# The last moved pair of the second attention is cast half a tile later, GpSimd takes half of two low parts, and the last early output step stands between the last transposes

## The chip, the cores and the metric

The program runs on one core of one Trainium2 chip. The metric is the device time of one execution in microseconds (us); lower is better. A core has five instruction queues that matter here: PE (TensorE, matmuls and transposes), ACT (ScalarE), DVE (VectorE), POOL (GpSimd) and SP (SyncE, which only issues DMAs). Each works through its own instructions in the order in which they were written into its queue, and waits for others by semaphores.

## The reference, cut to what matters

Two layers over 1024 rows of width 1024: differential attention, then multi-head latent attention (MLA), each with a gate, an output projection and a residual. The change is at the end of the second one:

```python
sc = (jnp.einsum('bqhd,bkhd->bhqk', qn, k_nope, preferred_element_type=f32)
      + jnp.einsum('bqhr,bkr->bhqk', qp, k_pe, preferred_element_type=f32)) * scale
p = jax.nn.softmax(sc, axis=-1)
return jnp.einsum('bhqk,bkhd->bqhd', p.astype(v.dtype), v)
...
o = o.reshape(b, s, MLA_WIDTH) * jax.nn.silu(z)
return o @ w_out
```

There are 8 heads with 1024 queries and 1024 keys each. All is float32. The kernel gets there by splitting an operand x into a high part (a cast to the matmul's float32r) and a low part (x minus the high part), and adding three matmuls: high x high, high x low, low x high (`mm3`, L203 to L205).

## The kernel before

**Tiles.** `attn1` (from L1839) goes through one head in 8 tiles of 128 queries. A counter `now[0]` runs on over the heads, so tile n is tile n - 8h of head h: head 6 has the tiles 48 to 55, head 7, the last, 56 to 63. For a tile, `scores1` does ten score matmuls into PSUM (the tile `s1`, printed as `s`; six on `kn`, then four on `kps`), DVE takes the negated row maximum (`nm`, L433), ACT the exponential (`e`, L436).

**Transposes.** The weights e have to be transposed before the product with v (`pv`). There are two ways:
- by PE, in two halves of four 128x128 transposes (`tr`, L414, `Tail.turn(0)` and `turn(1)`). ACT casts the half to its high part (`pth<-tr`, L416), DVE subtracts for the low part (`ptl<-tr`, L419). There is one PSUM buffer for `tr`, so the next half on PE can begin only when DVE has done the low part of the one before. Tile n's first half is transposed after the scores of tile n+1, its second half amid the scores of tile n+2, between their six `kn` matmuls and their four `kps` matmuls.
- by moving ("moved pair", class `Mate`), in heads 0 to 6 for tiles 0, 1 and for tiles 4, 5: DVE transposes 32x32 blocks (`eT`, L1047), the result goes to DRAM (`pS`) and comes back rearranged (`pr`, four DMAs, `Mate.fetch`). Then `Mate.high` has ACT cast two blocks of 128x1024 (`pth<-pr`, L1065), one for each half kh of the keys, and `Mate.low` has the low parts done (`ptl<-pr`): by DVE (L1084), and for the very last pair, whose `high` runs with `closing[0]` set, by GpSimd for kh = 0 (L1081).

**When.** `settle` sets the steps by tile number: a pair that ends in tile n is fetched at n+2, its `high` at n+4 (`SPLIT_AT`), its `low` at n+5, its product at n+6 (one later for head 6's first pair). So head 6's first pair (tiles 48, 49) has `high` at tile 53, `low` at 54 and its product at 56; its last pair (tiles 52, 53) has `high` at 57, `low` at 58 and its product at 59. In heads 0 to 6 these steps are written right behind the tile's scores; in head 7 behind all of the tile's other work. Head 7 has no moved pairs. While it runs, `closing[0]` is set and the casts on ACT and the exponentials keep the order in which the program has them (`pin_last`); PE's order is fixed throughout (`pin`). Instructions on DVE, POOL and SP are put in order by the scheduler, with hints (`behind`, `in_turn`).

**The end.** During head 7, `extra1` also loads what the output projection needs and, by the table `PRE1` (one entry a tile from 56 on, then three for the end), does early steps of the output projection: six matmuls `oacc` for one head (`Pre.step`). After tile 63, `run_tails` does the last three half transposes (tile 62's second half, tile 63's first and second) with an `extra1` call behind each, and then tile 63's product:

```python
        prev.turn(1)
        fill(0)
        last.turn(0)
        prev.pv(0)
        prev.pv(1)
        fill(1)
        last.turn(1)
        fill(2)
        last.pv(0)
        last.pv(1)
```

Here `fill(i)` is `extra(8 + i)`, and `prev.pv` does nothing, since the product of two tiles is done with the second of them.

## Time and profile before

| | us |
|---|---|
| three runs | 1411.88, 1419.05, 1419.73 |
| their median | 1419.05 |
| the profiled execution, its own time | 1413.83 |
| its span, first to last instruction | 1412.0 |
| PE busy in the span | 1374.9 |

The profiled execution took 1.83 us more than its span. The scores of the tiles that matter start on PE at (tile: us) 54: 1251.87, 55: 1254.88, 56: 1257.54, 57: 1264.99, 58: 1271.05, 59: 1280.08, 60: 1287.13, 61: 1293.18, 62: 1299.24, 63: 1304.53; the last product starts at 1318.34.

A row of the timeline has its start, its length, the engine, the line, the operation with output and input, and in brackets the idle time of the engine before it and what ended that. A group "x2" is two instructions, from the start of the first to the end of the second. Matmul rows overlap: a 128x512 matmul is shown some 0.4 us long, but the next one starts about 0.23 us after it.

### The profile page before, as it was taken

What the parts mean: (1) busy time and instruction counts of PE and PEld (TensorE: products, weight loads), DVE (VectorE), ACT (ScalarE), POOL (GpSimd) and SP (SyncE); (2) the same over time, 40 slices, a digit from 0 to 9 for tenths busy, and PEclk for the clock granted to TensorE, in tenths of its full rate; (3) what the DMA queues carried; (4) which work ended last, traced back from release to release, by engine and by line L of the source; (5) the groups of instructions that cost most, each with busy time, mean ns of one, the idle gap of its engine ahead of it and who ended that gap; (6) DMA issues with size and microseconds to landing.
All of it is one profiled execution on the core that took longest, in us unless ns stands there. A gap on an engine that the chain in (4) does not pass through costs nothing.

```text
span 1412.0 us, 20440 instructions
## 1 busy us (share of the span) xinstructions
PE 1374.9 (97%) x7254; PEld 1150.0 (81%) x7254; DVE 936.7 (66%) x1365; ACT 740.3 (52%) x1290; POOL 610.6 (43%) x484
## 2 busy tenths in 40 slices
PE   9999899999999999999999999999999999998997
PEld 7778688888888888787778878888888888887886
DVE  7756687676777767678445787346777776764455
ACT  6623366666565655566443654345555555644342
POOL 4415164646564646462563235513142432313662
PEclk9999999999999999999999999999999999999999
DMA  9877723233333232336672222448688787776663
GB/s 352 262 226 233 237 66 103 79 103 83 105 85 95 80 96 81 97 87 221 219 240 97 97 90 90 126 146 261 164 223 248 213 240 195 204 214 214 226 213 129
DMA packets 147736, 230.98 MB, mean 164 GB/s; under 512 B 19121, under 2 KB 70449, under 8 KB 147634
## 3 DMA queue, kind: packets, MB, share of 16 engines
q1 hardware_dynamic: 147634, 229.68, 53.5%
q8 instruction: 57, 0.93, 0.3%
q14 instruction: 45, 0.37, 0.1%
HBM read 145.79 MB, written 60.23 MB: 146 GB/s over the span
## 4 chain that ended last, share of the span: by engine, by line
PE 78%; DMA 7%; DVE 6%; issue 3%; ACT 3%; SPq 2%; POOL 1%; ACTq 0%; POOLq 0%; DVEq 0%
PE acc L203 9%; PE acc L205 9%; PE acc L204 9%; PE s L1831 8%; PE s L905 7%; PE tr L414 6%; PE pv L204 4%; PE pv L205 4%; PE pv L203 4%; PE oacc L204 3%; PE oacc L205 3%; PE oacc L203 3%; PE zacc L203 1%; PE zacc L205 1%; PE zacc L204 1%
## 5 line engine op out<-in xcount | busy, mean ns | idle before, releaser
L433 DVE TENSOR_REDUCE nm<-s 128x1 f32<-128x1024 f32 x192 | 234.0, 1219 | 87.8 <-PE s L905 66.6
L416 ACT CAST pth<-tr 128x512 fp32r<-128x512 f32 x200 | 117.4, 587 | 212.8 <-PE tr L414 211.9
L436 ACT ACTIVATE e<-s,nm 128x1024 f32<-128x1024 f32 x128 | 143.2, 1119 | 94.6 <-DVE nm L433 94.2
L419 DVE TENSOR_TENSOR ptl<-tr,pth 128x512 fp32r<-128x512 f32 x200 | 137.2, 686 | 75.8 <-ACT pth L416 75.7
L254 POOL TENSOR_TENSOR wl<-wraw,wh 128x512 fp32r<-128x512 f32 (+2 forms) x82 | 102.7, 1254 | 170.4 <-ACT wh L253 162.8
L203 PE MATMUL acc<-h0h,wh 128*128 128x512 f32 x360 | 151.6, 421 | 1.8 <-DVE v_hl L393 1.7
L203 PE MATMUL pv<-pth,vt 128*128 128x256 f32 x512 | 146.4, 286 | 0.0
L204 PE MATMUL pv<-ptl,vt 128*128 128x256 f32 x512 | 145.2, 284 | 0.1
L205 PE MATMUL pv<-pth,vt 128*128 128x256 f32 x512 | 144.5, 282 | 0.0
L205 PE MATMUL acc<-h0h,wl 128*128 128x512 f32 x360 | 143.3, 398 | 0.1
L204 PE MATMUL acc<-h0l,wh 128*128 128x512 f32 x360 | 142.4, 396 | 0.0
L414 PE MATMUL tr<-ident,e 128*128 128x128 f32 x800 | 120.9, 273 | 10.1 <-DVE ptl L419 10.0
L414 PEld LDWEIGHTS tr<-ident,e 128*128 128x128 f32 x800 | 96.2, 140 | 41.6 <-DVE ptl L419 16.3
L1234 POOL TENSOR_TENSOR wol<-wor,woh 128x512 fp32r<-128x512 f32 x64 | 86.6, 1372 | 77.4 <-ACT woh L1233 71.4
L204 PEld LDWEIGHTS pv<-ptl,vt 128*128 128x128 f32 x512 | 97.2, 190 | 5.1 <-DVE ptl L419 0.4
L203 PEld LDWEIGHTS pv<-pth,vt 128*128 128x128 f32 x512 | 97.0, 189 | 4.5 <-ACT pth L416 0.4
L205 PEld LDWEIGHTS pv<-pth,vt 128*128 128x128 f32 x512 | 97.6, 191 | 0.1
L905 PE MATMUL s<-ks,qa 128*128 128x512 f32 x256 | 82.7, 403 | 6.0 <-ACT e L436 3.0
L913 DVE SCALAR_TENSOR_TENSOR e<-s,z,e 128x1024 f32<-128x1024 f32 x64 | 82.1, 1283 | 2.1
L355 POOL TENSOR_TENSOR rp_sw<-rp_sw,sinT 128x512 f32<-128x512 f32 x42 | 55.3, 1316 | 62.8 <-DMA rp_sw<-rp_raw 57.6
L205 PEld LDWEIGHTS acc<-h0h,wl 128*128 128x128 f32 x360 | 68.3, 190 | 16.4 <-POOL wl L254 0.6
L905 PE MATMUL s<-ks,qb 128*128 128x512 f32 x256 | 81.1, 396 | 0.0
(632 smaller groups left out, 3442.2 us busy)
## 6 DMA issues: line engine op xcount, KB each, us to landing
ada<-in_ada_ss SPq DMA_DIRECT2D x32, 512.0 KB, 6.4
wraw<-in_w_s SPq DMA_DIRECT2D x64, 256.0 KB, 2.8
vS<-v_hl SPq DMA_DIRECT2D x32, 512.0 KB, 5.0
vt<-vS SPq DMA_DIRECT2D x32, 512.0 KB, 5.0
wor<-in_w_out SPq DMA_DIRECT2D x64, 256.0 KB, 4.2
pS<-eT SPq DMA_DIRECT2D x28, 512.0 KB, 2.9
pr<-pS SPq DMA_DIRECT2D x56, 256.0 KB, 6.2
rp_sw<-rp_raw SPq DMA_DIRECT2D x168, 64.0 KB, 2.0
```

The lines of the kernel that those rows point to most:

```text
L203: pin(PE.matmul(psum, ah, bh, start=first, stop=False))
L204: pin(PE.matmul(psum, ah, bl, start=False, stop=False))
L205: mm = PE.matmul(psum, al, bh, start=False, stop=last)
L254: sub = (lo_on or (V if pair_of else G)).tensor_sub(l_[:, :n], raw[:, :n], f32v(h_[:, :n]))
L414: pin(PE.transpose(tr[:, j, :], p[:, kt * P : (kt + 1) * P], ident))
L416: cp = S.copy(pth[kh][:, :, dst], tr)
L419: mk["V"] = V.tensor_sub(ptl[kh][:, :, dst], tr, f32v(pth[kh][:, :, dst])).ins
L433: mk["V"] = V.reduce_max(nm, s_ps, axis=AX.X, negate=True).ins
L436: ex = S.activation(e, s_ps, AF.Exp, bias=nm, scale=1.0, accum_out=zs)
L905: PE.matmul(s_ps[:, kc * HF : (kc + 1) * HF], src[:, c, ql], KS[h][kc][:, c, :], start=fst, stop=not fst)
L1234: in_turn(G.tensor_sub(lo, raw, f32v(hi)))
L1831: pin(PE.matmul(s_ps[:, kc * HF : (kc + 1) * HF], lhs, rhs(kc), start=i == 0, stop=i == 4))
```

## The change

Three edits.
- `Mate.high` in head 7 (that is the last moved pair's, at tile 57) does nothing itself but leaves its work, now called `spread`, in a list `swing`. `scores1` of tile 58 runs it amid the scores, right after the second half transpose of tile 56. `low` stays at tile 58, behind its other work.
- Both of head 6's pairs now have their kh = 0 low part done by GpSimd, in `spread`, and their kh = 1 low part by DVE, in `low`. Before, this held for the last pair alone, and both were issued in `high` then; the first pair's two low parts were both DVE's.
- `PRE1` has its last early step one place earlier: between tile 63's first half transpose and its second, not behind the second.

```diff
-PRE1 = (0, 0, 1, 0, 0, 0, 1, 1, 1, 0, 1)
+PRE1 = (0, 0, 1, 0, 0, 0, 1, 1, 1, 1, 0)
...
-            self.done = False
+            self.onG = int(c["h"] == NH - 2)
...
         def high(self):
+            if closing[0]:
+                swing.append(self.spread)
+            else:
+                self.spread()
+
+        def spread(self):
             self.pt = alloc_pt(self.c["pt"])
             for kh in range(2):
-                r, (hi, _) = self.views(kh)
+                r, (hi, lo) = self.views(kh)
                 with behind("S"):
                     cp = S.copy(hi, r)
                     pin_last(cp)
                     last = cp.ins
+                if kh < self.onG:
+                    in_turn(G.tensor_sub(lo, r, f32v(hi)))
             mk["S"] = last
-            if closing[0]:
-                self.low(G)
-            else:
+            if not closing[0]:
                 mk["H"] = last
 
-        def low(self, eng=V):
-            if eng is V and self.done:
-                return
-            self.done = True
-            for kh in range(2):
+        def low(self):
+            for kh in range(self.onG, 2):
                 r, (hi, lo) = self.views(kh)
-                if eng is G and kh == 0:
-                    in_turn(G.tensor_sub(lo, r, f32v(hi)))
-                else:
-                    with behind("V"):
-                        V.tensor_sub(lo, r, f32v(hi))
-
-    tails, hooks = [None, None], []
+                with behind("V"):
+                    V.tensor_sub(lo, r, f32v(hi))
+
+    tails, hooks, swing = [None, None], [], []
...
-            if i == SPL1 and tails[0]:
-                tails[0].turn(1)
+            if i == SPL1:
+                if tails[0]:
+                    tails[0].turn(1)
+                while swing:
+                    swing.pop(0)()
```

What this moves in the queues. ACT around tiles 57 and 58, before. The first row is the cast of tile 56's first half, the `pth<-pr` pair is the last moved pair's, the `pth<-tr` behind it is tile 56's second half, and `s1_12870` are the scores of tile 58:

```order
L416 CAST pth_12826<-tr_12830 128x4x128
L1884 CAST bc_s_12520<-o1_12781 128x512
L1065 CAST pth_12851<-pr_12659 128x1024
L1065 CAST pth_12852<-pr_12659 128x1024
L1233 CAST woh_12859<-wor_12783 128x512
L416 CAST pth_12827<-tr_12877 128x4x128
L436 ACTIVATE e_12890,zz1_12725<-s1_12870,nm_12888 128x1024
```

The same place after the change (tile 58's scores are now `s1_12862`):

```order
L416 CAST pth_12826<-tr_12830 128x4x128
L1887 CAST bc_s_12520<-o1_12781 128x512
L1233 CAST woh_12851<-wor_12783 128x512
L416 CAST pth_12827<-tr_12869 128x4x128
L1071 CAST pth_12876<-pr_12659 128x1024
L1071 CAST pth_12877<-pr_12659 128x1024
L436 ACTIVATE e_12889,zz1_12725<-s1_12862,nm_12887 128x1024
```

The two moved casts went behind `woh` and behind the cast of tile 56's second half, and still stand ahead of tile 58's exponential.

DVE at the same place, before; `nm_12888` is tile 58's maximum, `ptl_12829<-tr_12877` the low part of tile 56's second half, `ptl_12828<-tr_12892` and `ptl_12829<-tr_12925` those of tile 57's halves:

```order
L433 TENSOR_REDUCE nm_12888<-s1_12870 128x1
L1084 TENSOR_TENSOR ptl_12854<-pr_12659,pth_12852 128x1024
L419 TENSOR_TENSOR ptl_12829<-tr_12877,pth_12827 128x4x128
L419 TENSOR_TENSOR ptl_12828<-tr_12892,pth_12826 128x4x128
L419 TENSOR_TENSOR ptl_12829<-tr_12925,pth_12827 128x4x128
L433 TENSOR_REDUCE nm_12936<-s1_12918 128x1
```

And after:

```order
L419 TENSOR_TENSOR ptl_12829<-tr_12869,pth_12827 128x4x128
L433 TENSOR_REDUCE nm_12887<-s1_12862 128x1
L419 TENSOR_TENSOR ptl_12828<-tr_12891,pth_12826 128x4x128
L1084 TENSOR_TENSOR ptl_12879<-pr_12659,pth_12877 128x1024
L419 TENSOR_TENSOR ptl_12829<-tr_12925,pth_12827 128x4x128
L433 TENSOR_REDUCE nm_12936<-s1_12918 128x1
```

Tile 56's low part moved ahead of tile 58's maximum, and the moved pair's low part from ahead of it to two places behind it. On POOL the first pair's low part is new, at tile 53, and the last pair's went from ahead of the first `wol<-wor` to behind it. On SP the load of head 7's second half of v (`vt`) went from behind the loads of `o1a3` and `o1a4` to ahead of them.

DVE at tiles 54 and 55, before; `nm_12645` is tile 54's maximum, `nm_12675` tile 55's, and the row behind that the low part of tile 54's first half:

```order
L433 TENSOR_REDUCE nm_12645<-s1_12634 128x1
L1084 TENSOR_TENSOR ptl_12596<-pr_12457,pth_12594 128x1024
L1084 TENSOR_TENSOR ptl_12597<-pr_12457,pth_12595 128x1024
L1777 SCALAR_TENSOR_TENSOR qn_l_12656<-acc_12566,qn_h_12655 128x512
L433 TENSOR_REDUCE nm_12675<-s1_12664 128x1
L419 TENSOR_TENSOR ptl_12681<-tr_12683,pth_12679 128x4x128
```

And after:

```order
L433 TENSOR_REDUCE nm_12646<-s1_12635 128x1
L1084 TENSOR_TENSOR ptl_12597<-pr_12457,pth_12595 128x1024
L433 TENSOR_REDUCE nm_12675<-s1_12664 128x1
L1777 SCALAR_TENSOR_TENSOR qn_l_12656<-acc_12566,qn_h_12655 128x512
L419 TENSOR_TENSOR ptl_12681<-tr_12683,pth_12679 128x4x128
```

One of the two low parts left DVE, and `qn_l` went behind tile 55's maximum.

PE after tile 63, as one piece of the difference; the `tr` row with x8 is tile 63's two halves, `o1a3` and `o1a4` are the last two early steps, `pv` the last product:

```order
 L204 MATMUL oacc<-wol,o1a3h 128x512
 L205 MATMUL oacc<-woh,o1a3l 128x512
-L414 MATMUL tr<-ident,e 128x128 x8
+L414 MATMUL tr<-ident,e 128x128 x4
 L203 MATMUL oacc<-woh,o1a4h 128x512
 L204 MATMUL oacc<-wol,o1a4h 128x512
```

The last four transposes went behind the six matmuls of the early step, directly ahead of `pv`.

## The prediction

> **What bounds the kernel now.** I read the page first, for the engine that sets the time, then the list of waits for the stretch that the change touches, then its timeline row by row.

> ```profile
> PE 1374.9 (97%) x7254; PEld 1150.0 (81%) x7254; DVE 936.7 (66%) x1365; ACT 740.3 (52%) x1290; POOL 610.6 (43%) x484
> ...
> PE 78%; DMA 7%; DVE 6%; issue 3%; ACT 3%; SPq 2%; POOL 1%; ACTq 0%; POOLq 0%; DVEq 0%
> ```

> PE is busy in 97% of the span, and the chain that ended last runs over PE for 78% of it. The change takes no matmul away, so it can bring only what PE loses to waits and to a lower clock. From 1225 us to the end of the span, PE's list of waits has one line (total, times, longest):

> ```profile
> PE tr L414 <- DVE ptl L419: 6.9, 5, 3.7
> ```

> So 6.9 us is all there is to take in waits: five times PE stood before a half transpose until DVE had done the low part of the half before, which frees the one `tr` buffer. The timeline has the five:

> ```profile
> 1260.27 0.65 PE L414 MATMUL tr<-ident,e 128*128 128x128 f32 x4 [1.11 <-DVE ptl L419]
> ...
> 1277.66 0.63 PE L414 MATMUL tr<-ident,e 128*128 128x128 f32 x4 [3.71 <-DVE ptl L419]
> ...
> 1302.64 0.66 PE L414 MATMUL tr<-ident,e 128*128 128x128 f32 x4 [0.48 <-DVE ptl L419]
> ...
> 1306.27 0.66 PE L414 MATMUL tr<-ident,e 128*128 128x128 f32 x4 [0.22 <-DVE ptl L419]
> ...
> 1316.45 0.66 PE L414 MATMUL tr<-ident,e 128*128 128x128 f32 x4 [1.40 <-DVE ptl L419]
> ```

> In order these are tile 56, tile 58, tiles 62 and 63, and the last transpose. The three edits aim at the first, second and fifth. Behind the second stands a further loss:

> ```profile
> 1272.44 0.60 PE L414 MATMUL tr<-ident,e 128*128 128x128 f32 x4
> ...
> 1280.08 1.05 PE L1831 MATMUL s<-kn_h,qn_h 128*128 128x512 f32 x2
> ...
> 1282.47 0.60 PE L414 MATMUL tr<-ident,e 128*128 128x128 f32 x4
> ...
> 1300.64 0.60 PE L414 MATMUL tr<-ident,e 128*128 128x128 f32 x4
> ...
> 1304.53 0.61 PE L1831 MATMUL s<-kn_h,qn_h 128*128 128x512 f32 x2
> ```

> The same view by stretches of 10 us (the third number from the end is the granted clock):

> ```profile
> 1280.00:1290.00 10.00, 10.00 (x58) 8.67 (x57) 3.51 (x6) 2.86 (x5) 0.82 (x1) 0.89 0.55 192
> ```

> Two score matmuls take 1.05 us at 1280.08 and 0.61 us at 1304.53, and the clock was 0.89: after the long wait PE ran slowly for a while.

> **Edit 1, the casts half a tile later.** Why did tile 58 wait 3.71 us? ACT and DVE there:

> ```profile
> 1272.36 1.99 ACT L1065 CAST pth<-pr 128x1024 fp32r<-128x1024 f32 x2 [0.60 <-issue]
> ...
> 1274.78 0.58 ACT L416 CAST pth<-tr 128x512 fp32r<-128x512 f32 x1
> ...
> 1275.14 1.78 DVE L1084 TENSOR_TENSOR ptl<-pr,pth 128x1024 fp32r<-128x1024 f32 x1
> 1276.84 0.68 DVE L419 TENSOR_TENSOR ptl<-tr,pth 128x512 fp32r<-128x512 f32 x1
> ```

> The transpose of 1272.44 is tile 56's second half. Its cast came only at 1274.78, behind the two moved casts (and a `woh`), and its low part at 1276.84, behind the moved pair's low part. After the change both stand ahead of those. What the place then looks like, tile 62 shows: it has the same PE program (transpose, four `kps`, transpose, six `oacc`, six `kn` of the next tile, transpose) and no moved pair. There the three transposes start at 1300.64, 1302.64 and 1306.27, which is 5.63 us from first to last. At tile 58 they start at 1272.44, 1277.66 and 1282.47, which is 10.03. If tile 58 becomes like tile 62, the gain is 10.03 - 5.63 = **4.40 us**: 3.22 up to the second transpose (5.22 against 2.00), and 1.18 behind it, where the slow stretch goes. Does it go with the wait? No slow matmul follows the wait of 1.40 us or the shorter ones (0.61 at 1304.53, 0.48 and 0.28 behind 1316.45 below), so I take it that it does; if it came from something else, the term would be 3.2. [...]

> Do the casts now hurt elsewhere? They stand between the cast of tile 56's half and tile 58's exponential, and tile 62 shows the room there:

> ```profile
> 1301.28 0.59 ACT L416 CAST pth<-tr 128x512 fp32r<-128x512 f32 x1 [1.32 <-PE tr L414]
> ...
> 1303.81 1.12 ACT L436 ACTIVATE e<-s,nm 128x1024 f32<-128x1024 f32 x1 [1.95 <-DVE nm L433]
> ```

> ACT idles 1.95 us before the exponential, waiting for the maximum; the pair of casts takes 1.99 us by its row, some 1.9 from start to start of what follows. They just fit: 0 to 0.1 us. Of the DMA they no longer need anything: the four `pr` loads had landed when the casts began at 1272.36, and the casts now begin about 1.2 us later than that (0.6 behind the transpose of 1272.44 the cast of its half, 0.5 behind that the moved ones). GpSimd's kh = 0 low part:

> ```profile
> 1273.48 2.35 POOL L1081 TENSOR_TENSOR ptl<-pr,pth 128x1024 fp32r<-128x1024 f32 x1 [0.36 <-DMA o1a1l<-oS]
> ...
> 1306.09 1.28 POOL L1234 TENSOR_TENSOR wol<-wor,woh 128x512 fp32r<-128x512 f32 x1 [3.29 <-ACT woh L1233]
> ```

> It now comes behind a `wol` of 1.28 us, which fits before the first moved cast is done, and is finished some 4.6 us after tile 56's transpose; the product that needs it starts 6.9 after it (5.63, a transpose, four `kps`). DVE's kh = 1 low part now stands between the low parts of tile 57's two halves. With 1.78 us, as at 1275.14, it pushes the second of them and tile 59's maximum by half a microsecond. What that meets, tiles 59 and 60 show:

> ```profile
> 1284.34 1.21 DVE L433 TENSOR_REDUCE nm<-s 128x1 f32<-128x1024 f32 x1
> ...
> 1287.36 0.69 DVE L419 TENSOR_TENSOR ptl<-tr,pth 128x512 fp32r<-128x512 f32 x1 [0.30 <-ACT pth L416]
> ...
> 1288.53 0.60 PE L414 MATMUL tr<-ident,e 128*128 128x128 f32 x4
> ```

> Tile 59's maximum starts, exponential and cast follow, the low part is done at 1288.05, and PE wants the buffer at 1288.53: 0.48 us of slack. So the push is absorbed but for 0 to 0.1 us. I take **0.1 us** off for both.

> [...]

> **Edit 2, half of the first pair's low part on GpSimd.** Tile 56 waited for this row chain on DVE:

> ```profile
> 1255.53 2.35 DVE L1084 TENSOR_TENSOR ptl<-pr,pth 128x1024 fp32r<-128x1024 f32 x2
> 1257.80 0.69 DVE L1777 SCALAR_TENSOR_TENSOR qn_l<-acc,qn_h 128x512 fp32r<-128x512 f32 x1
> 1258.40 1.22 DVE L433 TENSOR_REDUCE nm<-s 128x1 f32<-128x1024 f32 x1
> 1259.53 0.68 DVE L419 TENSOR_TENSOR ptl<-tr,pth 128x512 fp32r<-128x512 f32 x1
> ```

> and the end of tile 55's scores on PE:

> ```profile
> 1256.72 0.63 PE L1831 MATMUL s<-kps,qpb 128*128 128x512 f32 x2
> ```

> One L1084 goes, so DVE is free at 1255.53 + 1.17 = 1256.70. Next is tile 55's maximum, whose scores end at 1257.35, so it runs 1257.40 to 1258.53 (start to start 1.13), then `qn_l` to 1259.13, then the low part, done 0.68 later at 1259.81 against 1260.21: **0.40 us**, not the 1.17 us that left DVE, because the scores are now late. If `qn_l` did not stand in between, it would be the whole 1.0; if GpSimd got in the way of the maximum, nothing: 0 to 1.0. GpSimd has the time:

> ```profile
> 1258.12 1.54 POOL L1864 TENSOR_TENSOR gz<-gz,bc_s 128x512 f32<-128x512 f32 x1 [8.99 <-DMA bc_s<-bc_d]
> ```

> It idled 8.99 us before this row; the new low part, 2.35 us long, lies inside that, and ends before DVE begins its own.

> **Edit 3, the early step between the last transposes.** The wait of 1.40 us at 1316.45 is bound by cast and low part of the transpose before, and nothing stood beside it. The six `oacc` that followed now fill it; they took 1316.87 to 1318.34, so they fit. What they covered is open then: the product's second half needs the last low part, and has only twelve `pv` ahead of it.

> ```profile
> 1316.87 0.48 PE L203 MATMUL oacc<-woh,o1a4h 128*128 128x512 f32 x1
> ...
> 1317.76 0.69 DVE L419 TENSOR_TENSOR ptl<-tr,pth 128x512 fp32r<-128x512 f32 x1 [1.37 <-ACT pth L416]
> ...
> 1318.34 0.28 PE L203 MATMUL pv<-pth,vt 128*128 128x256 f32 x1
> ```

> `pv` starts at 1316.87 then, its twelve take about 1.43, the first that needs the low part comes at 1318.42, and the low part ends at 1318.45: a wait of 0.1. So 1.40 - 0.1 = **1.3 us** (1.0 to 1.4). The step's own weights are there: the `wol` at 1306.09 (above) is its, and follows ACT's order when all comes earlier. Nothing waits on PE from there to the end by the list of waits, and the loads of the next weights and rows wait for that product, so they come earlier with it.

> **Sum.** 4.40 - 0.1 + 0.40 + 1.3 = 6.0 us. The profiled execution took 1413.83 us, which gives **1407.8**, say 1408. The three runs spread over 8 us, and their median of 1419.05 is 5.2 above the profiled execution, one of them 1.95 below it. I forecast for an execution like the profiled one, since only its rows can be argued with; if the new runs spread as the old ones did, their median is 1413.

> **The rivals.** (a) *Only a part comes.* SP now has head 7's second `vt` ahead of four `o1a` loads. Before, it was issued at 1285.45 (after tile 59's first twelve `pv`), landed 5.0 us later and was used at 1291.67:

> ```profile
> 1285.45 0.32 SPq L405 DMA_DIRECT2D vt<-vS  x1
> ...
> 1291.67 0.36 PE L203 MATMUL pv<-pth,vt 128*128 128x256 f32 x1
> ...
> vt<-vS SPq DMA_DIRECT2D x1, 512.0 KB, 5.0
> ...
> DMA to landing us min/median/max: 3.6/6.5/8.6
> ```

> It keeps 6.2 us, but four loads of 256 KB now crowd in behind it; at the worst landing of this stretch, 8.6, PE waits 2.4 us at tile 60. That gives 1410.2. For it: the slack is only 1.2 us. Against it: those four are issued later than it. The other part that may fall out is the slow stretch: if it stays without the wait, 1409.0.

> (b) *The wait moves to tile 59.* If the two casts begin late, tile 58's exponential, the cast of tile 57's half and the third transpose move with them, one for one: then 3.22 us come back there, and only 1413.83 - 6.0 + 3.2 = 1411.0 is left, or nothing if another slow stretch follows. Against it: 0.15 us of room, and work ahead of them that tile 62 shows on time.

> (c) *Slower.* The casts now stand ahead of tile 58's exponential in ACT's fixed order, so a late `pr` blocks the softmax itself. Before, the landing set when they began:

> ```profile
> 1258.05 2.60 SPq L1054 DMA_DIRECT2D pr<-pS x4
> ...
> DMA to landing us min/median/max: 3.4/7.4/11.4
> ```

> From the last issue, near 1260.2, they must land within some 13.5 us not to cost anything; 11.4 is the worst row. Every microsecond beyond is lost once, and beyond 19.5 the gain of 6.0 is gone; at 21 and with a new slow stretch of 1.2 it would be 1416.5. It needs the loads to be nearly twice as slow, while one competitor, `o1a0l`, now comes behind them.

> **How the numbers follow.** Forecast 0.68, (a) 0.19, (b) 0.09, (c) 0.04. The terms' bounds: at the least edit 1 brings 4.40 - 0.1 - 1.18 (the slow stretch stays) - 2.4 (`vt`) = 0.7, edit 2 nothing, edit 3 1.0, together 1.7; at the most edit 1 5.1 (tile 62's own two waits of 0.48 and 0.22 gone too), edit 2 1.0, edit 3 1.4, together 7.5. From the profiled execution that is 1406.3 to 1412.1. The runs lie from 1.95 below to 5.9 above it, which widens this to 1404.4 and 1418; the uppermost 2 us need the worst of every term in the longest of the runs, so the range is 1404.5 to 1416. One per cent, 14 us, is about what a measurement of this kernel can tell from no change. No case reaches it by its terms; faster by over 1% needs the spread of the runs on top: 0.05. Slower by over 1%: 0.02. Within: 0.93.

> **What would show it.** In the trace after: at tile 58 no wait over 0.6 us before the second transpose and no clock under 1.00 behind it; the three transposes 5.6 to 5.8 us apart in all; PE's wait at tile 56 near 0.7; `pv` right behind the last transpose with 0.1 us of wait inside. I am wrong if tile 59 or 60 gets a wait of over 1 us, if `pr` or `vt` is what ends a wait, or if the slow stretch shows up in another place.

## The result, and the profile after

| | before | after |
|---|---|---|
| median of 7 runs each, us | 1414.67 (1411.88 to 1419.73) | 1407.04 (1404.94 to 1409.20) |
| profiled execution, us | 1413.83 | 1405.69 |
| its span, us | 1412.0 | 1403.9 |

The ratio of after to before is 0.9955, with a 95% interval of 0.994 to 0.997. A second measurement (below) gave 0.9954, 0.9937 to 0.9972: the change saves some 6.4 us, less than half a per cent. The forecast was 1408.0.

The tile numbers in this text count from the second attention's first tile (`now[0]` itself runs on from the first layer, so that tile 58 here is 122 there). The page of the kernel after, its engines:

```profile
PE 1372.2 (98%) x7254; PEld 1148.3 (82%) x7254; DVE 933.8 (67%) x1364; ACT 740.5 (53%) x1290; POOL 612.9 (44%) x485
```

The matmuls are the same 7254. What went is waiting; PE's list of waits from 1225 us to the end (total, times, longest) now reads:

```profile
PE tr L414 <- DVE ptl L419: 2.1, 5, 0.7
```

It was 6.9 us with 3.7 as the longest. In PE's timeline the places are these, first tile 56, then the three transposes of tile 58 with a pair of score matmuls among them:

```profile
1257.22 0.66 PE L414 MATMUL tr<-ident,e 128*128 128x128 f32 x4 [0.68 <-DVE ptl L419]
...
1269.39 0.60 PE L414 MATMUL tr<-ident,e 128*128 128x128 f32 x4
...
1271.40 0.66 PE L414 MATMUL tr<-ident,e 128*128 128x128 f32 x4 [0.49 <-DVE ptl L419]
...
1273.29 0.62 PE L1831 MATMUL s<-kn_h,qn_h 128*128 128x512 f32 x2
...
1275.03 0.66 PE L414 MATMUL tr<-ident,e 128*128 128x128 f32 x4 [0.22 <-DVE ptl L419]
```

Tile 58's second wait fell from 3.71 to 0.49 us, the pair of score matmuls takes 0.62 us instead of 1.05, and the three transposes stand 5.64 us apart instead of 10.03. The granted clock (third number from the end) stays at full there:

```profile
1270.00:1280.00 10.00, 9.29 (x58) 7.72 (x58) 6.08 (x7) 6.81 (x11) 7.48 (x5) 1.00 0.58 203
```

At the end the last transpose no longer waits, and the product stands right behind it:

```profile
1307.01 0.66 PE L414 MATMUL tr<-ident,e 128*128 128x128 f32 x4
...
1309.07 0.66 PE L414 MATMUL tr<-ident,e 128*128 128x128 f32 x4
...
1312.55 0.39 PE L203 MATMUL oacc<-woh,o1a5h 128*128 128x512 f32 x1
```

The runs of one kernel spread over some 4 to 12 us, so the experiments are read by a **stretch** of the timeline: from tile 55's first score matmul to the first output matmul of `o1a5h`, behind the last product. It runs from 1254.88 to 1321.20 before (66.32 us) and from 1252.24 to 1312.55 after (60.31 us). All three edits lie in it.

### The profile page after: what moved, and what is told of

Same layout as the page of the kernel before. It is cut to its first block, busy times and chain, and to the rows that moved or that the text cites. A ratio compares the mean times of both kernels' runs of the same rounds, so it can differ in the third digit from the quotient of the medians.

```text
span 1403.9 us, 20442 instructions
## 1 busy us (share of the span) xinstructions
PE 1372.2 (98%) x7254; PEld 1148.3 (82%) x7254; DVE 933.8 (67%) x1364; ACT 740.5 (53%) x1290; POOL 612.9 (44%) x485
## 4 chain that ended last, share of the span: by engine, by line
PE 81%; DVE 6%; DMA 4%; ACT 3%; issue 3%; SPq 1%; POOL 1%; ACTq 0%; POOLq 0%; DVEq 0%
PE s L1831 9%; PE acc L203 9%; PE acc L205 9%; PE acc L204 9%; PE s L905 7%; PE tr L414 6%; PE pv L204 4%; PE pv L205 4%; PE pv L203 4%; PE oacc L203 4%; PE oacc L205 4%; PE oacc L204 4%; PE zacc L203 1%; PE zacc L205 1%; PE zacc L204 1%
## 5 line engine op out<-in xcount | busy, mean ns | idle before, releaser
L433 DVE TENSOR_REDUCE nm<-s 128x1 f32<-128x1024 f32 x192 | 233.9, 1218 | 84.8 <-PE s L905 65.1
L416 ACT CAST pth<-tr 128x512 fp32r<-128x512 f32 x200 | 117.5, 587 | 208.4 <-PE tr L414 207.5
L436 ACT ACTIVATE e<-s,nm 128x1024 f32<-128x1024 f32 x128 | 143.3, 1120 | 94.0 <-DVE nm L433 93.5
L419 DVE TENSOR_TENSOR ptl<-tr,pth 128x512 fp32r<-128x512 f32 x200 | 137.2, 686 | 74.3 <-ACT pth L416 74.3
L203 PE MATMUL acc<-h0h,wh 128*128 128x512 f32 x360 | 151.2, 420 | 1.3 <-DVE v_hl L393 0.9
L203 PE MATMUL pv<-pth,vt 128*128 128x256 f32 x512 | 146.4, 286 | 0.0
L414 PEld LDWEIGHTS tr<-ident,e 128*128 128x128 f32 x800 | 96.1, 140 | 38.3 <-DVE ptl L419 17.4
L414 PE MATMUL tr<-ident,e 128*128 128x128 f32 x800 | 121.0, 273 | 6.3 <-DVE ptl L419 6.1
L1234 POOL TENSOR_TENSOR wol<-wor,woh 128x512 fp32r<-128x512 f32 x64 | 86.8, 1375 | 75.7 <-ACT woh L1233 64.3
L203 PEld LDWEIGHTS pv<-pth,vt 128*128 128x128 f32 x512 | 97.0, 189 | 4.5 <-ACT pth L416 0.4
## 6 DMA issues: line engine op xcount, KB each, us to landing
ada<-in_ada_ss SPq DMA_DIRECT2D x32, 512.0 KB, 6.4
vS<-v_hl SPq DMA_DIRECT2D x32, 512.0 KB, 5.0
vt<-vS SPq DMA_DIRECT2D x32, 512.0 KB, 5.1
pS<-eT SPq DMA_DIRECT2D x28, 512.0 KB, 2.9
```

What stands on the lines that cost most here:

```text
L203: pin(PE.matmul(psum, ah, bh, start=first, stop=False))
L414: pin(PE.transpose(tr[:, j, :], p[:, kt * P : (kt + 1) * P], ident))
L416: cp = S.copy(pth[kh][:, :, dst], tr)
L419: mk["V"] = V.tensor_sub(ptl[kh][:, :, dst], tr, f32v(pth[kh][:, :, dst])).ins
L433: mk["V"] = V.reduce_max(nm, s_ps, axis=AX.X, negate=True).ins
L436: ex = S.activation(e, s_ps, AF.Exp, bias=nm, scale=1.0, accum_out=zs)
```

## The experiments

All were compared with the kernel before on the same chip. "Stretch" is worked out from the starts of those two rows in each kernel's profiled execution.

| kernel | stretch, us | ratio to before, 95% interval |
|---|---|---|
| before, three profiled executions | 66.32, 67.15, 67.08 | |
| after, two profiled executions | 60.31, 60.31 | 0.9955 (0.994 to 0.997), 0.9954 (0.9937 to 0.9972) |
| moved casts alone | 62.00 | 0.9976 (0.9964 to 0.9987) |
| GpSimd's share in the first pair alone | 65.45 | 0.9983 (0.9972 to 0.9993) |
| last tile's early step alone | 63.07 | 0.9976 (0.9962 to 0.999) |
| before, the wait filled | 64.46 | 0.9985 (0.9974 to 0.9996) |
| after, casts ahead of the half transpose | 62.97 | 0.998 (0.9967 to 0.9993) |
| after, low part all on VectorE | 61.85 | 0.9968 (0.9951 to 0.9985) |
| after, casts a whole tile later | 66.33 | 0.9992 (0.9977 to 1.0007) |
| after, three more moves, twice | 58.88, 58.90 | 0.9949 (0.9933 to 0.9966), 0.9941 (0.9925 to 0.9958) |

**The moved casts alone.** The change without its line of `PRE1`, and with the first pair's low part left to DVE:

```diff
-            self.onG = int(c["h"] == NH - 2)
+            self.onG = int(c["h"] == NH - 2 and qp == 2)
```

> The kernel before with the moved casts alone; GpSimd's share and the early step of the last tile stay as before. Theory (the three edits act at three separate waits and add up): the three transposes of tile 58 stand about 5.6 us apart in all instead of 10.0 and run at full speed, the wait of tile 56 stays at 1.1 us and the one before the last transpose at 1.4 us; the stretch from tile 55's first score matmul to the first output matmul of o1a5h is 66.32 - 4.4 = 61.9 us. Rival (the casts need GpSimd's new share or the step to pay): a wait stays at tile 58 or appears at tile 59, and the stretch is 63 to 65 us.

Its timeline on PE (tile 56, the three transposes of tile 58, the last transpose):

```profile
1260.34 0.66 PE L414 MATMUL tr<-ident,e 128*128 128x128 f32 x4 [1.11 <-DVE ptl L419]
...
1272.52 0.60 PE L414 MATMUL tr<-ident,e 128*128 128x128 f32 x4
1274.52 0.66 PE L414 MATMUL tr<-ident,e 128*128 128x128 f32 x4 [0.48 <-DVE ptl L419]
1278.15 0.66 PE L414 MATMUL tr<-ident,e 128*128 128x128 f32 x4 [0.22 <-DVE ptl L419]
...
1312.20 0.66 PE L414 MATMUL tr<-ident,e 128*128 128x128 f32 x4 [1.40 <-DVE ptl L419]
```

The three transposes are 5.63 us apart, while the waits of 1.11 and 1.40 are those of before. The stretch is 4.32 us shorter, close to the theory's 4.4, and the casts need neither of the other edits.

**GpSimd's share alone.** In the kernel before, the first pair's first half goes to GpSimd behind its cast:

```diff
-                r, (hi, _) = self.views(kh)
+                r, (hi, lo) = self.views(kh)
...
+                if kh == 0 and self.c["h"] == NH - 2 and not closing[0]:
+                    in_turn(G.tensor_sub(lo, r, f32v(hi)))
...
-            for kh in range(2):
+            for kh in range(int(self.c["h"] == NH - 2 and not closing[0]), 2):
```

> The kernel before with GpSimd taking the first half of the first pair's low part (the part due at tile 56) and nothing else. Theory: the wait of tile 56 falls from 1.1 to about 0.7 us, tile 58 keeps its 3.7 us wait and the slow matmuls behind it, and the stretch from tile 55's first score matmul to the first output matmul of o1a5h is 66.32 - 0.4 = 65.9 us. Rival (the wait of tile 56 shrank only because the casts had moved as well): the wait stays at 1.1 us and the stretch at 66.3 us.

```profile
1258.72 0.66 PE L414 MATMUL tr<-ident,e 128*128 128x128 f32 x4 [0.68 <-DVE ptl L419]
...
1270.88 0.60 PE L414 MATMUL tr<-ident,e 128*128 128x128 f32 x4
1275.71 1.08 PE L414 MATMUL tr<-ident,e 128*128 128x128 f32 x4 [3.31 <-DVE ptl L419]
1280.46 0.60 PE L414 MATMUL tr<-ident,e 128*128 128x128 f32 x4
```

Tile 56's wait falls to 0.68 by this edit alone. From the stretch's start to tile 58's first transpose it takes 17.13 us (1253.75 to 1270.88) against 17.56 before: 0.43 saved, as expected. But the stretch lost 0.87. The other 0.44 went at tile 58, which the edit does not touch: its wait was 3.31 instead of 3.71, and the slow matmuls began at once (four transposes in 1.08 us) and were over sooner.

**The early step alone.** `PRE1` as in the change, nothing else.

> The kernel before with the early step of the last tile put between its last two transposes and nothing else. Theory: the 1.4 us wait before the last transpose is filled, from the last tile's third transpose to the end of the output it takes 7.0 - 1.3 = 5.7 us, and the stretch from tile 55's first score matmul to the first output matmul of o1a5h is 66.32 - 1.3 = 65.0 us, with tile 58 as before. Rival (the step is only moved within a chain that the softmax's tail sets): the wait moves to the product's first matmul and the stretch stays at 66.3 us.

```profile
1270.65 0.60 PE L414 MATMUL tr<-ident,e 128*128 128x128 f32 x4
...
1275.48 0.63 PE L414 MATMUL tr<-ident,e 128*128 128x128 f32 x4 [3.31 <-DVE ptl L419]
...
1278.71 0.60 PE L414 MATMUL tr<-ident,e 128*128 128x128 f32 x4
...
1312.70 0.65 PE L414 MATMUL tr<-ident,e 128*128 128x128 f32 x4
...
1316.17 0.39 PE L203 MATMUL oacc<-woh,o1a5h 128*128 128x512 f32 x1
```

The last transpose does not wait, and from the last tile's first half transpose (1310.64) to the end of the stretch it takes 5.53 us, against 6.81 (1314.39 to 1321.20) before: 1.28 saved. The stretch, however, lost 3.25 us. The rest, 1.97, again is tile 58, which nothing had touched: 8.06 us between its outer transposes instead of 10.03. The wait of 3.31 us is there, and **no slow matmul follows it**. The clock in the 10 us around it:

```profile
1274.00:1284.00 10.00, 8.52 (x55) 7.74 (x56) 4.43 (x7) 4.12 (x8) 4.65 (x3) 1.00 0.58 221
```

Of the single edits then, the first by its stretch and the other two read where they act, 4.32 + 0.43 + 1.28 = 6.03 us, and the whole change 6.01. By their total times they give more (0.9976, 0.9983 and 0.9976, so some 9 us); the intervals of the second and third even leave out the terms read in the trace. What the rest of these times is, the runs don't settle; tile 58's slow matmuls, which came out shorter or not at all in these two profiles, are one candidate.

**Filling the wait.** In the kernel before, 14 matmuls with no use stand in tile 58's wait:

```diff
+N_FILL = 14
...
+        if between and now[0] == 122:
+            kn_ = KN[NH - 1][0][0]
+            pre1.fill(N_FILL, kn_[:, :P], kn_)
...
+            for _ in range(n):
+                pin(PE.matmul(self.accs[0], lhs, rhs, start=True, stop=True))
```

> The kernel before with 14 more matmuls (about 3.3 us on TensorE, into a bank that is overwritten later, so that nothing uses them) put into the 3.7 us wait of tile 58, ahead of its second transpose. Theory (TensorE's idle wait is what brings the slow matmuls behind it): the wait left is about 0.4 us, the pairs of score matmuls behind it run at 0.6 us instead of 1.05, the clock's share stays at 1.00 there, and the stretch from tile 55's first score matmul to the first output matmul of o1a5h is 66.32 - 1.2 = 65.1 us although TensorE has more to do. Rival (the slow matmuls come from something else, such as the transfers and the other engines' load at that place): the wait is filled, the pairs still take 1.05 us and the stretch stays at 66.3 us.

(The lines are shifted by one or more in this kernel.)

```profile
1277.56 3.35 PE L1255 MATMUL oacc<-kn_h 128*128 128x512 f32 x14
1281.12 0.63 PE L415 MATMUL tr<-ident,e 128*128 128x128 f32 x4 [0.22 <-DVE ptl L420]
```

3.35 us of matmuls more, the wait 0.22, full speed behind it (0.63 us for the four transposes), and a stretch 1.86 us shorter. PE's work is not what this place costs. The gain is 0.7 us over the theory's 1.2: the first two transposes are 0.30 us closer (4.92 against 5.22), and the second and third 1.55 (3.26 against 4.81). Tile 62, from which the 1.2 was taken, has 3.63 there, with a wait of 0.22 in it that does not arise here. On the cause of the slow matmuls it says less than I wanted, since the run before this one had none of them with its wait unfilled.

**The kernel before again.** So it was profiled twice more, unchanged.

> The kernel before, unchanged, profiled once more. Theory A (the slow matmuls behind tile 58's wait come with the wait in every execution): the wait is 3.3 to 3.7 us, the pairs of score matmuls behind it take 1.05 us, and the stretch from tile 55's first score matmul to the first output matmul of o1a5h is 66.3 us, or 65.9 where the wait is 3.3 us. Theory B (whether they come is a matter of when the wait falls, as the kernel with the last tile's step alone suggests, where a 3.31 us wait was followed by matmuls at full speed): in some executions the stretch is 64.3 to 64.8 us, with pairs of 0.62 us.

> The kernel before, unchanged, profiled a third time. As for the second time: 65.9 to 66.3 us for the stretch and 1.05 us pairs by theory A; by theory B 64.3 to 64.8 us and pairs of 0.62 us in some executions, and more than one length of stretch among the three.

The second execution at tile 58, with the low part of DVE that the wait ends on:

```profile
1272.57 0.60 PE L414 MATMUL tr<-ident,e 128*128 128x128 f32 x4
...
1275.27 1.38 DVE L1084 TENSOR_TENSOR ptl<-pr,pth 128x1024 fp32r<-128x1024 f32 x1
...
1277.40 1.09 PE L414 MATMUL tr<-ident,e 128*128 128x128 f32 x4 [3.31 <-DVE ptl L419]
...
1283.40 0.61 PE L414 MATMUL tr<-ident,e 128*128 128x128 f32 x4
```

10.83 us from first to last, 10.79 in the third execution. The wait was 3.31 in both; the 3.71 of the first was DVE's low part, 1.78 us long there and 1.38 here. To see the slow part, the same view in windows of half a microsecond at its two edges (third number from the end: the granted clock), the first execution:

```profile
1278.50:1279.00 0.50, 0.50 (x4) 0.85 1.04 402
1282.00:1282.50 0.50, 0.50 (x3) 0.74 0.47 180
```

and the second:

```profile
1276.50:1277.00 0.50, 0.00 (x0) 0.58 1.05 401
1283.00:1283.50 0.50, 0.50 (x3) 0.59 0.00 0
```

All between was at 0.50. A clock of 0.85 in a window means half rate in 0.30 of it, so the first ran at half rate from 1278.85 to 1282.26, 3.41 us, and the second from 1276.58 to 1283.41, 6.83 us: one piece of 3.41, and two. The third had two as well, the kernel with GpSimd's share one, the one with the early step none. Neither text fits as written. Slow matmuls came behind the wait in all three executions, but the stretches of the last two, 67.15 and 67.08 us, are longer than theory A has them, and the 64.3 to 64.8 us of theory B did not appear among the three. That the slow matmuls can stay away rests on the profile of the early step's kernel alone. Between its outer transposes tile 58 took 8.06, 9.58, 10.03, 10.79 and 10.83 us in five executions of the same code there, and 5.64 and 5.63 where the casts are moved. What decides between these is worked out below, behind the casts a whole tile later.

**Casts ahead of the half transpose.** In the kernel after, the order within tile 58's scores is turned round:

```diff
             if i == SPL1:
-                if tails[0]:
-                    tails[0].turn(1)
                 while swing:
                     swing.pop(0)()
+                if tails[0]:
+                    tails[0].turn(1)
```

> The kernel after, but in the second half of tile 56's step the moved casts of the last pair stand ahead of the second half of tile 58's transposes on ScalarE instead of behind them (same half tile, other order). Theory (ScalarE is what ends the second wait, and the order within the half tile matters): the second transpose of tile 58 waits 1.4 to 1.9 us instead of 0.5, the three transposes stand about 6.5 us apart instead of 5.64, and the stretch from tile 55's first score matmul to the first output matmul of o1a5h is 60.3 + 0.9 = 61.2 us. Rival (only the half tile matters, not the order in it): 60.3 us.

PE at tile 58, then ACT, whose second row is the cast of tile 56's second half:

```profile
1270.70 0.60 PE L414 MATMUL tr<-ident,e 128*128 128x128 f32 x4
...
1274.22 0.63 PE L414 MATMUL tr<-ident,e 128*128 128x128 f32 x4 [2.01 <-DVE ptl L419]
...
1279.05 0.60 PE L414 MATMUL tr<-ident,e 128*128 128x128 f32 x4
```

```profile
1270.43 2.00 ACT L1071 CAST pth<-pr 128x1024 fp32r<-128x1024 f32 x2
1272.32 0.59 ACT L416 CAST pth<-tr 128x512 fp32r<-128x512 f32 x1
```

The half's cast starts 1.62 us behind its transpose instead of 0.64 (1270.03 against 1269.39 in the kernel after). The wait is 2.01, a little over what was expected, but the three transposes stand 8.35 us apart instead of 6.5, and the stretch is 2.66 us longer instead of 0.9: a piece of half rate stands behind this wait as well (1.05 us for a pair at 1276.64). The order within the half tile matters, and the expectation lacked the clock.

**The low part all on VectorE.** In the kernel after:

```diff
-            self.onG = int(c["h"] == NH - 2)
+            self.onG = int(c["h"] == NH - 2 and qp == 0)
```

> The kernel after, but VectorE makes both halves of the last pair's low part and GpSimd none of it. Theory (GpSimd's share there has little worth once the casts stand where they are): small waits at tiles 59 and 60, together 0.3 to 0.6 us, and a stretch from tile 55's first score matmul to the first output matmul of o1a5h of 60.6 to 60.9 us. Rival (VectorE would be the bound of this place without GpSimd): waits of over 1 us at tile 59 or in the third transpose of tile 58, and 61.5 us or more.

PE, and DVE's two low parts:

```profile
1283.62 0.39 PE L204 MATMUL pv<-ptl,vt 128*128 128x256 f32 x1 [0.53 <-DVE ptl L1084]
...
1285.36 0.66 PE L414 MATMUL tr<-ident,e 128*128 128x128 f32 x4 [0.17 <-DVE ptl L419]
```

```profile
1281.25 3.45 DVE L1084 TENSOR_TENSOR ptl<-pr,pth 128x1024 fp32r<-128x1024 f32 x2
```

The stretch is 1.54 us longer, 2.5 to 5 times the expected: the product's first half waits inside, since the low part is now late for `pv` too, and DVE is 3.45 us in one piece. By the starts of the matmuls the first of these waits costs 0.79 us, not the 0.53 in its bracket: from 1282.82 to 1283.85 PE starts two matmuls, which takes 0.24 us elsewhere in that product. No single wait is over 1 us, so neither text fits wholly; the size is the rival's.

**A whole tile later.** In the kernel after, casts and low part run amid tile 59's scores:

```diff
-                swing.append(self.spread)
+                swing.extend([self.spread, self.low])
...
-                while swing:
+                while swing and now[0] == 123:
```

> The kernel after, but the last pair's casts and low part stand one tile later, amid tile 59's scores. Theory (half a tile is about all the delay that the low part's chain can bear): TensorE waits about 3.3 us at tile 59 for the casts and GpSimd's half of the low part, perhaps with slow matmuls behind it, and the stretch from tile 55's first score matmul to the first output matmul of o1a5h is 60.3 + 3.3 to 4.5 = 63.6 to 64.8 us. Rival (there is slack for a whole tile): 60.3 us, or 0.5 us less where the waits of tile 58 go as well.

```profile
1277.29 0.39 PE L203 MATMUL pv<-pth,vt 128*128 128x256 f32 x1 [0.69 <-ACT pth L1071]
...
1279.71 0.58 PE L204 MATMUL pv<-ptl,vt 128*128 128x256 f32 x1 [2.04 <-POOL ptl L1075]
```

2.73 us of wait in the two places that the theory named, and two pieces of half rate; in the 10 us around them:

```profile
1278.00:1288.00 10.00, 8.29 (x39) 7.96 (x40) 4.14 (x5) 2.18 (x5) 1.65 (x1) 0.66 0.44 153
```

A clock of 0.66 over 10 us is 6.8 us at half rate. The stretch is 6.02 us longer than after and equal to that of before. The stretch lies above the 63.6 to 64.8 us expected: the waits were right, but the clock costs more than they do (6.02 - 2.73 = 3.29 us).

**Where a wait falls.** Whether a wait brings slow matmuls can be read from the traces on hand. All profiles but one (the second with the three more moves) also have two pieces of half rate, together 6.83 us, near 154 us. Their start is read as above; here for the kernel before, first execution,

```profile
155.50:156.00 0.50, 0.00 (x0) 0.00 (x0) 0.50 (x2) 0.06 (x1) 0.00 (x0) 0.86 0.82 221
```

and for the kernel with the early step alone:

```profile
153.50:154.00 0.50, 0.50 (x4) 0.26 (x2) 0.50 (x1) 0.00 (x0) 0.00 (x0) 0.99 0.53 205
```

They start at 155.86 and 153.99. From 155.86 to the piece at 1278.85 it is 1122.99 us, which is 329.0 times 3.4133, the length that one profile gives by itself (the second of the kernel after has pieces from 566.68 and 976.28, 120 such lengths apart). In each profile the later pieces begin a whole number of 3.4133 us behind the first, to within 0.01 us in twelve cases: in these profiles the pieces lie on one grid through the whole execution. Call 3.4133 us of it, from edge to edge, a period. PE's waits at tiles 58 and 59 can then be cut at these edges:

| kernel | first piece | piece at tile 58 or 59 | periods between | PE waits in the period ahead, us | and in the piece's first period, us | pieces |
|---|---|---|---|---|---|---|
| before, first execution | 155.86 | 1278.85 | 329.0 | 2.22 | 0 | 1 |
| before, second | 153.60 | 1276.58 | 329.0 | 2.49 | 0.82 | 2 |
| before, third | 154.39 | 1277.38 | 329.0 | 2.38 | 0.93 | 2 |
| GpSimd's share alone | 152.59 | 1275.58 | 329.0 | 3.18 | 0.13 | 1 |
| early step alone | 153.99 | none | edge at 1273.56 | 1.39, then 1.92 | | 0 |
| after, casts ahead of the half transpose | 152.45 | 1275.44 | 329.0 | 2.01 | 0 | 1 |
| after, casts a whole tile later | 152.71 | 1279.11 | 330.0 | 2.13 | 0.60 | 2 |

In these profiles half rate followed a period in which PE waited for 2.0 us or more, whether the wait itself was 2.01 or 3.71 us long. In the early step's kernel the edge cuts the wait of 3.31 us (1272.17 to 1275.48) nearly in the middle, and no period has that much. A second piece followed where at least 0.60 us of waits still lay in the first. The other periods of the fourteen profiles agree: of those at full rate each one with 2.0 us or more of waits is followed by half rate, none with less than 1.6 is, and in between both occur; and no first piece with 0.28 us or less in it has a second. By an estimate from the 1.92 us, which no half rate followed, a wait of 3.31 us escapes only where the edge falls into its middle half microsecond. If all places are equally likely, that is one in seven (0.5 of 3.41), so that before the change slow matmuls are the rule. In both profiles of the kernel after no period in the stretch has more than 0.9 us of waits.

**Three more moves.** In the kernel after, half of the early step stands ahead of the second transpose at tiles 58 and 62, and the exponential behind the next half's cast (the third move, DVE's `qn_l` behind the low part at tile 56, did not take place: DVE's order there is that of after):

```diff
+        if lead:
+            lead()
...
+        for f in hold:
+            f()
...
+                lead_ = late and qp * 2 + t in (2, 6)
+                hold = [] if lead_ else None
...
+                    after_scores(fill, 1, late, pre1.half if lead_ else None, hold or ())
```

> The kernel after, with three more moves of order: at tiles 58 and 62 half of the early output step stands ahead of the second transpose, the exponential stands behind the cast of the next half of the transposes, and VectorE's low part of the query of head 7's second half stands behind the low part due at tile 56. Theory (what is left of the waits of tile 58 is ScalarE's and VectorE's order, not their work): the three transposes of tile 58 stand about 4.5 us apart instead of 5.64, those of tile 62 lose about as much, and the time is 2 us below the kernel after. Rival (the work of ScalarE and VectorE in this stretch is the bound, so that a wait only moves): the transposes come closer and the same time is lost at tiles 59 to 60 or in the last product, with no change of the time.

> The kernel after, unchanged, timed on the same chip as the one with the three more moves and profiled again. Nothing of it waits over 0.7 us, so by both theories on the slow matmuls its stretch from tile 55's first score matmul to the first output matmul of o1a5h is 60.3 us within 0.1, with no pair over 0.65 us there; its time is 0.9955 of the kernel before within the spread of the runs.

> The kernel with the three more moves of order, timed again, beside the kernel after on one chip. Theory (its shorter stretch, 58.9 us against 60.3 us, is all that is to be had): 1.4 us below the kernel after in the median, which is of the size of the spread of the runs, so that the ratio to the kernel before should be 0.001 below the other's. Rival (the stretch differs by accident of the profiled execution): the stretch is 60 us or more here.

PE at tile 58 in the first of its executions:

```profile
1270.16 0.60 PE L414 MATMUL tr<-ident,e 128*128 128x128 f32 x4
...
1272.15 0.50 PE L204 MATMUL oacc<-wol,o1a0h 128*128 128x512 f32 x1 [0.23 <-POOL wol L1245]
...
1275.24 0.60 PE L414 MATMUL tr<-ident,e 128*128 128x128 f32 x4
```

The outer transposes are 5.08 us apart (expected 4.5); at tile 62, where nothing of this kind waits, they are 4.58. The 0.50 us between the two lie in the first gap (2.56 against 2.06), where the early step now waits for GpSimd's `wol`. Another 0.29 us is lost before tile 59's second transpose (3.56 us behind the first, 3.27 in the kernel after). The stretch is 58.88 and 58.90: 1.4 us below after, which came out at 60.31 again, and it repeats. On one chip the medians were 1406.15 for this kernel and 1409.15 for after. The ratios differ by 0.0013, less than either interval's half width, so by total time a gain over the kernel after is not shown.

## Why the prediction was right, point by point

- **Edit 1's wait** (3.22 us): 5.22 became 2.01 us up to the second transpose. Tile 62 as the pattern of the place after held to 0.01 us (5.64 against 5.63).
- **Edit 1's slow stretch** (1.18 us): right for the profiled execution, but the step behind it, that the slow matmuls come and go with the long wait, is only half true: the wait was 3.31 or 3.71 us in the five executions with tile 58 as before, and slow matmuls followed it for 3.41 us, for 6.83 us or not at all. Where they came, a period of the grid held 2.0 us or more of the wait. No wait that stays in the stretch is over 0.68 us, and none of these had slow matmuls behind it; but with the casts ahead of the half transpose a wait of 2.01 us had them. What the slow matmuls cost by themselves in that execution is 1.6 us (4.81 against 3.26 and 3.23 without them); the 1.18 is what is left when tile 62's own wait of 0.22 us comes in. By the outer transposes, edit 1 is worth 10.03 - 5.64 = 4.4 us against the profiled execution, and 2.4 to 5.2 us against the other four. The text put it at 3.2 if the slow stretch stayed, and at 5.1 at the most; that the slow stretch could be absent before the change, so that less is to be gained, was not among its cases, nor was a second piece.
- **The casts' cost** (0.1 us): ACT had no gap and none was lost:

```profile
1270.51 2.00 ACT L1071 CAST pth<-pr 128x1024 fp32r<-128x1024 f32 x2
1272.57 1.12 ACT L436 ACTIVATE e<-s,nm 128x1024 f32<-128x1024 f32 x1
```

 The exponential follows the casts at once. Some 0.06 us went instead from the third transpose to tile 59's first (2.85 against 2.79 before). DVE's moved low part took 1.74 us, near the 1.78 that was put in, but beside another operation of GpSimd: the 1.78 at 1275.14 lay beside the pair's kh = 0 half (1273.48 to 1275.83), while here that half had ended at 1274.04, and what ran was the product `gz` of 1273.99.
- **Edit 2** (0.40): 0.43, by the path that was worked out: DVE has one low part, waits for the scores, and `qn_l` still stands in between.

```profile
1252.89 1.22 DVE L1084 TENSOR_TENSOR ptl<-pr,pth 128x1024 fp32r<-128x1024 f32 x1
1254.74 1.23 DVE L433 TENSOR_REDUCE nm<-s 128x1 f32<-128x1024 f32 x1 [0.64 <-PE s L1831]
1255.88 0.68 DVE L1777 SCALAR_TENSOR_TENSOR qn_l<-acc,qn_h 128x512 fp32r<-128x512 f32 x1
```

- **Edit 3** (1.3): 1.28, with the last product right behind the transpose. The 0.1 us inside the product is there too: the first matmul that needs the last low part starts 0.15 us behind its neighbour (1311.13 against 1310.98) and the next one 0.22 us behind that, where 0.12 is usual.
- **The sum** (6.0): 6.01 in the stretch. That it fits so closely is luck in one respect: the prediction's profile was one with a single piece of half rate, and against the second and third execution of before the stretch is 6.84 and 6.77 us shorter. The two spans differ by 8.1; 2.64 us more had been gained before tile 55 (1254.88 against 1252.24), where the code is the same, and 0.55 was lost behind the stretch. That is the spread of executions: the second profile of the kernel after reached tile 55 at 1258.25, 6.0 us later than the first, with the same stretch to the hundredth.
- **The rivals**: (a) no wait for `vt` appeared at tile 60; (b) no wait appeared at tile 59 in the kernel after, while the one with the casts a whole tile later shows that it does, 2.73 us of it, once the room is used up; (c) the casts followed the half's cast without waiting for `pr`.
- **The level**: the forecast stood on the profiled execution, and the median after fell within a microsecond of it. That is luck in part: the saving by total time is some 6.4 us with an interval of 4.2 to 8.5, and the profiled execution was itself 0.8 us below the median of before. My remark that the median might be 1413 took the three runs shown for typical; four more of them brought the median of before down to 1414.67.

## What to carry to other kernels

Where work was put ahead of a softmax's chain on an in-order engine, look for a neighbouring tile with the same program and without that work: its rows gave the time after to 0.01 us here (5.63 against 5.64). Read a small change in the stretch that it touches and profile the unchanged kernel more than once, since a term can be an accident of one execution: here the same code took 8.06 to 10.83 us. A wait of PE can be worth more than its length: here 3.29 us more were lost behind waits of 2.73 us, and 1.6 behind one of 3.71 us, but nothing behind one of 3.31 us; it hung on how much of the wait fell into one period of 3.41 us.

## What the runs showed of the hardware that I had not expected

```profile
560.00:570.00 10.00, 8.21 (x34) 6.04 (x32) 8.07 (x10) 6.23 (x11) 5.49 (x5) 0.83 0.43 117
970.00:980.00 10.00, 8.30 (x29) 6.14 (x28) 3.94 (x6) 4.36 (x9) 3.95 (x4) 0.83 0.87 255
```

 They may be part of what makes runs of one kernel differ; that was not measured.
- A low part on DVE of 1.22 us alone (1252.89 in the kernel after, GpSimd idle) took 1.38 to 1.78 beside GpSimd in the kernel before, and 2.52 with the casts a whole tile later, where it lay beside GpSimd's low part:

```profile
1278.21 2.52 DVE L1084 TENSOR_TENSOR ptl<-pr,pth 128x1024 fp32r<-128x1024 f32 x1
```

 So in these profiles the same instruction took 1.1 to 2.1 times its own time beside GpSimd. In these three cases the excess (0.16, 0.56 and 1.30 us) is 0.13 to 0.14 less than the time for which the GpSimd operation begun before it still ran (0.30, 0.69 and 1.44). The 0.40 us between waits of 3.31 and 3.71 us is no more than that.
